# A Hymba layer on one core: the input projection with two products per weight tile in place of three

## The chip, the core and the metric

One core of a Trainium2 chip computes one layer of a hybrid decoder. TensorE (PE in the profile) multiplies; VectorE (DVE), ScalarE (ACT) and GpSimd (POOL) do the elementwise work; SyncE (SP) issues the loads of the weights. The metric is the time of one execution in microseconds (us); less is better.

## The reference

```python
def rms_norm(x, g):
    xf = x.astype(jnp.float32)
    y = xf * lax.rsqrt(jnp.mean(xf * xf, axis=-1, keepdims=True) + EPS)
    return (y * g.astype(jnp.float32)).astype(x.dtype)
...
        xn = rms_norm(h, g_mix[l])
        proj = xn @ w_in[l]
        lru_x, lru_gate, q, kc, vc, ksel, vsel, kw, vw, gate_logits = jnp.split(proj, cuts, axis=-1)
        u = causal_dwconv(lru_x, lru_conv_w[l], lru_conv_b[l])
        y_lru = rg_lru(u, lru_wa[l], lru_ba[l], lru_wx[l], lru_bx[l], lru_lambda[l]) * jax.nn.gelu(lru_gate)
...
        k_cmp = compress_kv(kc, cmp_pe_k[l], cmp_w1_k[l], cmp_b1_k[l], cmp_w2_k[l])
        v_cmp = compress_kv(vc, cmp_pe_v[l], cmp_w1_v[l], cmp_b1_v[l], cmp_w2_v[l])
        y_attn = nsa_attention(q, k_cmp, v_cmp, ksel, vsel, kw, vw, gate_logits)
        mixed = jnp.concatenate([rms_norm(y_lru, g_lru_out[l]), rms_norm(y_attn, g_attn_out[l])], axis=-1)
        h = h + mixed @ w_out[l]
        xn = rms_norm(h, g_ffn[l])
        u_ff, v_ff = jnp.split(xn @ w_up[l], 2, axis=-1)
        u_ff = causal_dwconv(u_ff, ffn_conv_w[l], ffn_conv_b[l])
        h = h + (jax.nn.gelu(u_ff) * v_ff) @ w_down[l]
    return rms_norm(h, g_final)
```

There are 256 tokens, a model width of 2048, eight query heads and two key heads of 128, a recurrent group (RG-LRU) of 1024 channels and a feed-forward width of 6144. All is float32.

## The kernel before

**The weight stream.** The four big matrices (w_in, w_out, w_up, w_down) and the compressor's weights pass once through the chip as a list of *parts*. A part is 1024 weights per partition: in the input projection four tiles of 128 input channels (*contraction tiles*) by 256 output columns. A group of four such parts makes 256 columns of the projection. Loads of one or two parts go through SP into three buffers (`raw`). Each part is split into two float32r halves of 12 bits (`emit_split`): ACT copies the high part (`hi`, L282), DVE subtracts it from the weights (`lo`, L283). There are four buffers of each; splitting runs two parts ahead of the products, loading five. The activations are split in the same way, in tiles `act` with a high and a low part of 256 columns (tokens) side by side.

**The products.** A product of two split numbers leaves out low x low. With the weights standing still and the tokens moving (`mm_weights_still_plain`, L312 to L323, used through `still_x`), a weight tile of 128 x 128 takes three products of 256 columns that add up in the first half of a PSUM bank: high weights x high activations (L320), high x low (L321), low x high (L322). Column tile m has bank m of a pair, and there are two pairs (`ps_mm`). This form serves 16 of the 18 groups of the input projection, 64 parts, 512 weight tiles. The up-projection has another form (`mm_weights_still`): the high weights meet both parts of the activations in one product over a whole bank (512 columns, L336), and the low weights go into its second half (256 columns, L339). Its evictions add the two halves (`halves`, L344 to L348: ACT copies the second half to `ev`, DVE adds the first). The output and down projections move the weights (`moving`, L365 to L367, 512 columns each).

**The order of the groups.** First the compressor's inputs, keys and values by turns (gk, gv); the keys of the selected branch (KS); the keys of the window (KW), by turns with the compressor's weights for keys; the first queries, by turns with the compressor's weights for values; values, the other queries; four groups of recurrent inputs (X) and four of gates (G); then the output projection, its attention rows and its recurrent rows. After a group's last part, `post` evicts its banks: `post_cmp_in` copies them (L418), `post_keys` (L485), `post_q`, `post_lru_x` and `post_lru_g` (L707) multiply them by the tokens' 1/rms, one DVE instruction each.

**Work beside the stream.** Side work (lanes of small tasks) is put between parts. One task sums the squares of x, makes 1/rms per token, and spreads it over the partitions with two products (L200) and a copy to `rsb` (`across`, L202). `blocks` then scales the compressor's inputs and lays out overlapping blocks (POOL, `kvc`, `kb`) and splits them (ACT L432, DVE L433, `kbs`); the compressor's products (L446) read `kbs`. The recurrence (L717 on) starts when the last group of gates has been evicted; its result and the squares of it go into the recurrent rows of the output projection.

**What sets the order.** The program is written in that order, but the Tile scheduler runs with a timeline of its own (`schedule_with_timeline_sim=True`) and orders each engine's instructions by it. So the instructions stand in another order than they are written in, and a change of one kind of work moves others.

Of the kernel before, what the change touches and what calls it, by code (L numbers as in the profile page):

```python
# [15 lines left out]
P = 128  # L16
S = 256            # tokens
NB = S // P        # token blocks
D = 2048
KT = D // P        # contraction tiles of the model width  # L20
# [5 lines left out]
NC = 15            # compressed blocks  # L26
CB = 32            # tokens of a compressed block
CS = 16            # its stride
# [4 lines left out]
LOAD = 2048        # elements per partition of one weight load  # L33
PART = 1024        # elements per partition that are split and multiplied at once
LOOK_LOAD = 5      # parts by which loads run ahead
LOOK_SPLIT = 2     # parts by which the splitting runs ahead
FF_CUT = 3         # the feed-forward width is worked through in so many pieces
PACE = 655         # pace of the side work: units per contraction tile of 256 columns that it is put between
TAIL = 8           # contraction tiles at the end that finish the first token block before the second
# [5 lines left out]
class Part:  # L45
    """A piece of the weight stream: its load, and what is done with it once it is on chip."""

    def __init__(self, load, k0, nk, cols, mm, post):
        self.load, self.k0, self.nk, self.cols = load, k0, nk, cols
        self.mm, self.post, self.pre = mm, post, None  # L50
        self.hi = self.lo = None


class Lane:
    """A queue of side tasks (generators that yield the distance to their next step, in units of PACE)."""
# [22 lines left out]
def hymba_block(ctx, tc, x, g_mix, w_in, lru_conv_w, lru_conv_b, lru_wa, lru_ba, lru_wx, lru_bx, lru_lambda,  # L78
# [23 lines left out]
    # ---------------------------------------------------------------- constants and per-channel vectors  # L102
    ident = cst.tile([P, P], F32, name="ident")
    make_identity(nc, ident)
    xr = resp.tile([P, NB, D], F32, name="xr")           # the residual stream, tokens on partitions
# [8 lines left out]
    # keeps the tensor engine warm until the first operands are there  # L114
# [33 lines left out]
    # a compressed block counts for token t once it has ended: 16 n + 31 <= t  # L148
# [23 lines left out]
    # ---------------------------------------------------------------- helpers  # L172
    def inv_sqrt(v, y):
        """y = 1/sqrt(v) for [P, w]: the reciprocal's root, and a Newton step."""
# [13 lines left out]
    def inv_rms(total, n, name):  # L188
        """1/sqrt(total/n + eps) for [P, w] sums of squares."""
# [753 lines left out]
```

## Time and profile before

| | |
|---|---|
| median of 3 runs | 1186.98 us (1184.58 to 1187.15) |
| span of the profiled execution | 1185.0 us |
| PE busy | 1169.7 us, 99% |
| DVE busy | 766.8 us, 65% |
| ACT busy | 593.1 us, 50% |
| POOL busy | 159.5 us, 13% |
| read from memory | 214.43 MB, 183 GB/s over the span |

A busy share is an average over stages; the chain of work that ended last and the waits of a stretch tell which engine sets the time there. The input projection takes about the first 278 us, the output projection follows to about 350 us, then the feed-forward part runs to the end.

### The profile page before, as it was taken

The page shows a single profiled execution, that of the slowest core. Times are in us where ns is not written, and L with a number is a line of the kernel's source. Part 1 is how long each engine was busy: PE and PEld are TensorE (multiplying, and loading weights), DVE is VectorE, ACT ScalarE, POOL GpSimd, SP SyncE. Part 2 cuts the span into 40 slices and gives each one's busy share as a digit, 9 for nine tenths or more (in the row PEclk, how much of TensorE's full clock was granted, in tenths as well). Part 3 has the DMA queues.
Part 4 walks back from the last instruction along what each step waited for, and adds up shares of the span by engine and source line. Part 5 has one row for each costly group of instructions (what it writes and reads, how often), then busy time and mean ns, then how long its engine had stood idle before and what let it go on. Part 6 is the DMA issues. An engine that isn't in the chain of part 4 may idle for free.

```text
span 1185.0 us, 16730 instructions
## 1 busy us (share of the span) xinstructions
PE 1169.7 (99%) x6727; PEld 1021.5 (86%) x6727; DVE 766.8 (65%) x981; ACT 593.1 (50%) x803; POOL 159.5 (13%) x181
## 2 busy tenths in 40 slices
PE   8999999999999999999999999999999999999997
PEld 8999999898788888888888888888888888888885
DVE  4775778779766766666454766666454666666554
ACT  5554546786446554444333444444333454445444
POOL 3210224113200110110000110110000110110000
PEclk8999999999999999999999999999999999999999
DMA  9676544354655555565556555565555565565562
GB/s 295 178 221 213 160 134 157 121 165 136 217 192 177 176 180 192 176 200 179 204 186 196 179 194 180 178 208 182 187 204 185 176 207 180 178 193 183 194 202 81
DMA packets 182397, 217.60 MB, mean 184 GB/s; under 512 B 4064, under 2 KB 147584, under 8 KB 182192
## 3 DMA queue, kind: packets, MB, share of 16 engines
q1 hardware_dynamic: 180928, 213.07, 55.2%
q0 software_dynamic: 1072, 2.41, 0.6%
q8 instruction: 52, 0.85, 0.3%
q10 hardware_dynamic: 320, 1.06, 0.2%
q14 instruction: 25, 0.20, 0.0%
HBM read 214.43 MB, written 2.10 MB: 183 GB/s over the span
## 4 chain that ended last, share of the span: by engine, by line
PE 91%; DVE 2%; ACT 0%; issue 0%; POOL 0%; DVEq 0%
PE mm L336 30%; PE mm L339 15%; PE mm L366 9%; PE mm L367 9%; PE mm L365 9%; PE mm L322 4%; PE mm L320 4%; PE mm L321 4%; PE s L578 1%; DVE lo L283 1%; PE s L366 1%; PE s L365 1%; PE s L367 1%; PE pt L613 1%; DVE act L223 0%; PE s L604 0%
## 5 line engine op out<-in xcount | busy, mean ns | idle before, releaser
L283 DVE TENSOR_TENSOR lo<-raw,hi 128x1024 fp32r<-128x1024 f32 (+1 forms) x403 | 516.7, 1284 | 294.7 <-ACT hi L282 294.4
L282 ACT ACTIVATE hi<-raw 128x1024 fp32r<-128x1024 f32 (+1 forms) x403 | 424.3, 1055 | 427.7 <-PE mm L367 183.8
L336 PE MATMUL mm<-act,hi 128*128 128x512 f32 x1536 | 539.0, 398 | 0.0
L339 PE MATMUL mm<-act,lo 128*128 128x256 f32 x1536 | 424.2, 281 | 0.0
L336 PEld LDWEIGHTS mm<-act,hi 128*128 128x128 f32 x1536 | 285.7, 188 | 66.6
L339 PEld LDWEIGHTS mm<-act,lo 128*128 128x128 f32 x1536 | 290.6, 189 | 4.5
L366 PE MATMUL mm<-lo,act 128*128 128x512 f32 (+2 forms) x544 | 206.2, 379 | 2.1 <-DVE lo L283 2.1
L367 PE MATMUL mm<-hi,act 128*128 128x512 f32 (+2 forms) x544 | 205.9, 379 | 0.0
L365 PE MATMUL mm<-hi,act 128*128 128x512 f32 (+2 forms) x544 | 205.8, 379 | 0.0
L320 PE MATMUL mm<-act,hi 128*128 128x256 f32 x512 | 147.3, 291 | 1.8 <-ACT act L222 0.9
L322 PE MATMUL mm<-act,lo 128*128 128x256 f32 x512 | 147.9, 290 | 0.6 <-DVE lo L283 0.5
L321 PE MATMUL mm<-act,hi 128*128 128x256 f32 x512 | 147.0, 288 | 0.4 <-DVE act L223 0.4
L366 PEld LDWEIGHTS mm<-lo,act 128*128 128x128 f32 x544 | 102.3, 188 | 22.5 <-DVE lo L283 3.8
L365 PEld LDWEIGHTS mm<-hi,act 128*128 128x128 f32 x544 | 102.3, 188 | 18.9 <-issue 0.4
L367 PEld LDWEIGHTS mm<-hi,act 128*128 128x128 f32 x544 | 102.3, 188 | 18.6
L352 POOL TENSOR_TENSOR up<-up,rsb 128x512 f32<-128x512 f32 x24 | 28.6, 1190 | 593.7 <-DVE up L348 508.4
L320 PEld LDWEIGHTS mm<-act,hi 128*128 128x128 f32 x512 | 98.2, 193 | 4.9 <-issue 2.1
L322 PEld LDWEIGHTS mm<-act,lo 128*128 128x128 f32 x512 | 98.8, 193 | 3.1 <-issue 1.8
L321 PEld LDWEIGHTS mm<-act,hi 128*128 128x128 f32 x512 | 98.9, 194 | 2.2 <-issue 1.2
L347 ACT COPY ev<-mm 128x512 f32<-128x512 f32 x48 | 28.2, 587 | 87.9 <-PE mm L336 87.8
L352 POOL TENSOR_TENSOR cv<-cv,rsb 128x512 f32<-128x512 f32 x24 | 38.7, 1611 | 21.7 <-ACT cv L793 21.7
L348 DVE TENSOR_TENSOR v<-mm,ev 128x512 f32<-128x512 f32 x24 | 16.6, 692 | 29.5 <-ACT ev L347 29.5
(238 smaller groups left out, 740.0 us busy)
## 6 DMA issues: line engine op xcount, KB each, us to landing
raw<-in_w_up_dram SPq DMA_DIRECT2D x96, 1024.0 KB, 5.2
raw<-in_w_down_dram SPq DMA_DIRECT2D x48, 1024.0 KB, 5.1
raw<-in_w_in_dram SPq DMA_DIRECT2D x26, 1024.0 KB, 5.3
raw<-in_w_out_dram SPq DMA_DIRECT2D x16, 1024.0 KB, 5.1
raw<-in_w_in_dram SPq DMA_DIRECT2D x15, 512.0 KB, 5.1
xr<-in_x_dram SPq DMA_DIRECT2D x4, 512.0 KB, 7.5
raw<-in_cmp_w_k_dram SPq DMA_DIRECT2D x4, 512.0 KB, 5.5
raw<-in_cmp_w_v_dram SPq DMA_DIRECT2D x4, 512.0 KB, 5.3
```

The lines of the kernel that those rows point to most:

```text
L282: act(hi[:, :n], src, AF.Copy)
L283: tt(lo[:, :n], src, hi[:, :n].bitcast(F32), op=OP.subtract)
L320: mm(o, lhsT=wh, rhs=a[:, 0], start=k == 0, stop=False)
L321: mm(o, lhsT=wh, rhs=a[:, 1], start=False, stop=False)
L322: mm(o, lhsT=wl, rhs=a[:, 0], start=False, stop=k == kts - 1)
L336: both = lambda: mm(o, lhsT=wh, rhs=a.rearrange("p a s -> p (a s)"), start=k == 0, stop=last)
L339: mm(o[:, S:], lhsT=wl, rhs=a[:, 0], start=False, stop=False)
L347: nc.scalar.copy(t, ps[:, :, S:])
L352: nc.gpsimd.tensor_tensor(a, a, over_pair(shared[rs]), op=OP.mult)
L365: keep(mm(o, lhsT=h, rhs=p.hi[:, j], start=k == 0, stop=False))
L366: mm(o, lhsT=h, rhs=p.lo[:, j], start=False, stop=False)
L367: mm(o, lhsT=l, rhs=p.hi[:, j], start=False, stop=k == kts - 1)
```

## The change

`mm_weights_still_plain` gives way to `mm_weights_still_runs`. It multiplies as the up-projection does: high weights x both parts of the activations over a whole bank, low weights x high activations into the second half. In addition it orders a part's 16 products by kind: eight with high weights, eight with low; a new mark of the part, `lo_first`, lets every other part begin with its low ones, so that runs of neighbouring parts join. Since a bank now has two halves, all evictions of these groups add them: `scaled_halves` (a copy, an add and a multiply by 1/rms), or `halves` alone for the compressor's inputs. Comments have gone from the file too, so line numbers shift by 1 to 14 (L283 is L286 after, L202 is L203, L446 is L460, L717 is L731).

```diff
+        for i, p in enumerate(mine):
+            p.lo_first = i > 0 and (len(mine) - 1 - i) % 2 == 0
...
-    def mm_weights_still_plain(src):
+    def mm_weights_still_runs(src):
         def fn(p, j, k, st, kts):
             if k == 0:
                 st["ps"] = ps_mm.tile([P, 2, 512], F32, name="mm")
-            a = src(k)
-            for m in range(2):
-                o = st["ps"][:, m, :S]
-                wh, wl = p.hi[:, j, m * P:(m + 1) * P], p.lo[:, j, m * P:(m + 1) * P]
-                mm(o, lhsT=wh, rhs=a[:, 0], start=k == 0, stop=False)
-                mm(o, lhsT=wh, rhs=a[:, 1], start=False, stop=False)
-                mm(o, lhsT=wl, rhs=a[:, 0], start=False, stop=k == kts - 1)
+            tiles = [(i, m) for i in range(p.nk) for m in range(2)]
+            order = [(low,) + t for low in ((True, False) if p.lo_first else (False, True)) for t in tiles]
+            n = len(order) // p.nk
+            for low, i, m in order[j * n:(j + 1) * n]:
+                o, kk = st["ps"][:, m], p.k0 + i
+                a = src(kk)
+                w = (p.lo if low else p.hi)[:, i, m * P:(m + 1) * P]
+                if low:
+                    mm(o[:, S:], lhsT=w, rhs=a[:, 0], start=False, stop=False)
+                else:
+                    mm(o, lhsT=w, rhs=a.rearrange("p a s -> p (a s)"), start=kk == 0, stop=kk == kts - 1)
         return fn
...
+    def scaled_halves(dst, ps, rs):
+        halves(dst, ps)
+        tt(dst, dst, over_pair(shared[rs]), op=OP.mult)
...
-            nc.vector.tensor_copy(kvc[:, which], st["ps"][:, :, :S])
+            halves(kvc[:, which], st["ps"])
...
-            tt(kcat[:, :, br], st["ps"][:, :, :S], over_pair(shared["rsb"]), op=OP.mult)
+            scaled_halves(kcat[:, :, br], st["ps"], "rsb")
...
-            tt(qT[:, 2 * i:2 * i + 2], st["ps"][:, :, :S], over_pair(shared["rsbq"]), op=OP.mult)
+            scaled_halves(qT[:, 2 * i:2 * i + 2], st["ps"], "rsbq")
...
-            tt(xp[:, :, 3:], st["ps"][:, :, :S], over_pair(shared["rsb"]), op=OP.mult)
+            scaled_halves(xp[:, :, 3:], st["ps"], "rsb")
...
-            tt(gt, st["ps"][:, :, :S], over_pair(shared["rsb"]), op=OP.mult)
+            scaled_halves(gt, st["ps"], "rsb")
```

The order moves at three places. The first is DVE around the copy of 1/rms, `rsb`, while KS ends and KW begins (`sp` belongs to constants of the recurrence, `kcat` holds the evicted keys, `kbs` the compressor's blocks). Before:

```order
L537 SCALAR_TENSOR_TENSOR sp_1133<-sp_1133,sp_1131 128x8
L539 SCALAR_TENSOR_TENSOR sp<-sp_1133,sp_1130 128x8
L543 TENSOR_SCALAR sp_1152<-sp 128x8
L544 TENSOR_SCALAR sp4n<-sp 128x8
L202 COPY rsb<-pt 128x256
L283 TENSOR_TENSOR lo<-raw,hi 128x1024
L392 TENSOR_SCALAR rsbq<-rsb 128x256
L485 TENSOR_TENSOR kcat<-mm,rsb 128x2x256
L283 TENSOR_TENSOR lo<-raw,hi 128x1024 x2
L433 TENSOR_TENSOR kbs_160<-kb,kbs_160 128x32x30
```

And now:

```order
L187 TENSOR_TENSOR rs<-rms_r,rms_t 128x2
L409 TENSOR_SCALAR rsh<-rs 128x2
L357 TENSOR_TENSOR kcat<-mm,ev 128x2x256
L286 TENSOR_TENSOR lo<-raw,hi 128x1024 x2
L203 COPY rsb<-pt 128x256
L406 TENSOR_SCALAR rsbq<-rsb 128x256
L362 TENSOR_TENSOR kcat<-kcat,rsb 128x2x256
L286 TENSOR_TENSOR lo<-raw,hi 128x1024 x2
L447 TENSOR_TENSOR kbs_160<-kb,kbs_160 128x32x30
```

The copy of `rsb` (L202, now L203) stood ahead of a split and of the keys' eviction; now it stands behind the keys' add (L357) and two splits.

The second is PE at the same place. `mm_691` (now `mm_602`) is the accumulator of KW, `act` its activations, `hi` and `lo` the weights of a part by number; `s` takes the compressor's products. Before, from inside the compressor's first products on:

```order
L446 MATMUL s_722<-hi_762,kbs0_160 120x256
L446 MATMUL s_722<-lo_763,kbs0_160 120x256
L320 MATMUL mm_691<-act_397,hi_775 128x256
L321 MATMUL mm_691<-act_397,hi_775 128x256
L446 MATMUL s_722<-hi_805,kbs0_160 120x256
L322 MATMUL mm_691<-act_397,lo_776 128x256
```

Now, from the first part of KW on:

```order
L331 MATMUL mm_602<-act_179,hi_526 128x512 x8
L329 MATMUL mm_602<-act_179,lo_527 128x256 x8
L329 MATMUL mm_602<-act_231,lo_599 128x256 x3
L201 MATMUL pt_534<-ident_88,rs_503 128x128 x2
L329 MATMUL mm_602<-act_231,lo_599 128x256 x5
L331 MATMUL mm_602<-act_231,hi_598 128x512 x8
L331 MATMUL mm_602<-act_296,hi_635 128x512 x8
L329 MATMUL mm_602<-act_296,lo_636 128x256 x8
L329 MATMUL mm_602<-act_357,lo_671 128x256 x8
L331 MATMUL mm_602<-act_357,hi_670 128x512 x8
L460 MATMUL s_625<-hi_573,kbs0_160 120x256
L460 MATMUL s_625<-lo_574,kbs0_160 120x256
```

The two products that spread 1/rms (L201) stand behind the first part of KW and three products of its second, and all four parts of KW now come before the first compressor product (L460); before, the fourth (`hi_775`) came among the compressor's.

The third is DVE where the last gates are evicted and the recurrence begins (L717 and L731 are its first step, L724 and L738 the second, L727 and L741 the scan; L224 writes attention's result). Before:

```order
L283 TENSOR_TENSOR lo<-raw,hi 128x1024
L186 TENSOR_TENSOR rsA<-rms_r,rms_t 128x2
L717 SCALAR_TENSOR_TENSOR act<-act 128x4x256 x2
L283 TENSOR_TENSOR lo<-raw,hi 128x1024
L724 TENSOR_TENSOR act<-act 128x4x256 x2
L283 TENSOR_TENSOR lo<-raw,hi 128x1024
L727 SCALAR_TENSOR_TENSOR act<-act 128x256 x8
L283 TENSOR_TENSOR lo<-raw,hi 128x1024
L733 TENSOR_TENSOR gt_2933<-gt_2933,act 128x512
L707 TENSOR_TENSOR gt_3306<-mm,rsb 128x512
```

And now:

```order
L286 TENSOR_TENSOR lo<-raw,hi 128x1024
L224 SCALAR_TENSOR_TENSOR act<-s,vec,act 128x128
L731 SCALAR_TENSOR_TENSOR act<-act 128x4x256
L715 SCALAR_TENSOR_TENSOR act<-act,u 128x2x256
L286 TENSOR_TENSOR lo<-raw,hi 128x1024
L224 SCALAR_TENSOR_TENSOR act<-s,vec,act 128x128
L738 TENSOR_TENSOR act<-act 128x4x256
L714 SCALAR_TENSOR_TENSOR act<-gt_2383,act 128x2x256
L741 SCALAR_TENSOR_TENSOR act<-act 128x256 x3
L286 TENSOR_TENSOR lo<-raw,hi 128x1024
L741 SCALAR_TENSOR_TENSOR act<-act 128x256
```

Between two splits there stood two steps or the whole scan; now single steps stand there, with attention's last steps and those of the LRU gates (L714, L715) among them.

The loads on SP keep their order, and from about 300 us on all engines have the order they had.

## Rows read from the trace of the kernel before

**Rows 1.** The page: busy time by engine, and the chain's shares by engine.

```profile
PE 1169.7 (99%) x6727; PEld 1021.5 (86%) x6727; DVE 766.8 (65%) x981; ACT 593.1 (50%) x803; POOL 159.5 (13%) x181
...
PE 91%; DVE 2%; ACT 0%; issue 0%; POOL 0%; DVEq 0%
```

**Rows 2.** Windows: stretch, length, busy us (instructions) by engine, PEclk, DMA share, GB/s.

```profile
6.00:10.50 4.50, 3.22 (x17) 2.45 (x15) 2.76 (x5) 3.67 (x7) 3.09 (x7) 1.00 1.07 371
10.50:17.50 7.00, 6.49 (x31) 6.31 (x31) 1.91 (x4) 1.53 (x4) 2.28 (x7) 0.51 1.09 344
...
86.00:278.00 192.00, 192.00 (x1478) 181.12 (x1477) 138.31 (x232) 119.87 (x225) 42.02 (x53) 1.00 0.49 158
278.00:306.00 28.00, 25.93 (x110) 19.85 (x109) 28.00 (x34) 14.42 (x19) 15.61 (x15) 1.00 0.50 153
```

**Rows 3.** PE's timeline, last G part (48 products): start us, us, instruction.

```profile
272.08 0.28 PE L320 MATMUL mm<-act,hi 128*128 128x256 f32 x1
...
277.84 0.40 PE L365 MATMUL mm<-hi,act 128*128 128x512 f32 x1
```

**Rows 4.** The chain in order of time, up-projection, 32 weight tiles apart.

```profile
417.31 0.24 PE mm L339 x2
...
428.61 0.24 PE mm L339 x2
```

**Rows 5.** PE's timeline in the up-projection: two 512-column products in a row.

```profile
429.04 0.62 PE L336 MATMUL mm<-act,hi 128*128 128x512 f32 x2
429.50 0.28 PE L339 MATMUL mm<-act,lo 128*128 128x256 f32 x1
```

**Rows 6.** PE's timeline in the output projection: twelve 512-column products.

```profile
325.43 0.39 PE L365 MATMUL mm<-hi,act 128*128 128x512 f32 x1
...
328.15 0.39 PE L365 MATMUL mm<-hi,act 128*128 128x512 f32 x1
```

**Rows 7.** Groups by form: out<-in, shape, count, busy us, mean ns, idle before.

```profile
L347 ACT COPY ev<-mm 128x512 f32<-128x512 f32 x48 | 28.2, 587 | 87.9 <-PE mm L336 87.8
L348 DVE TENSOR_TENSOR up<-mm,ev 128x512 f32<-128x512 f32 x24 | 16.6, 692 | 29.0 <-ACT ev L347 29.0
L733 DVE TENSOR_TENSOR gt<-gt,act 128x512 f32<-128x512 f32 x4 | 2.7, 687 | 0.0
L707 DVE TENSOR_TENSOR gt<-mm,rsb 128x512 f32<-128x512 f32 x4 | 2.7, 682 | 0.1
```

**Rows 8.** Timelines of DVE, ACT and PE, 43 to 70 us.

```profile
43.87 1.23 DVE L283 TENSOR_TENSOR lo<-raw,hi 128x1024 fp32r<-128x1024 f32 x1 [0.20 <-ACT hi L282]
49.22 0.42 DVE L202 COPY rsb<-pt 128x256 f32<-128x256 f32 x1 [0.48 <-PE pt L200]
54.73 1.06 ACT L282 ACTIVATE hi<-raw 128x1024 fp32r<-128x1024 f32 x1 [1.77 <-PE mm L321]
59.09 1.16 DVE L433 TENSOR_TENSOR kbs<-kb,kbs 128x960 fp32r<-128x960 f32 x1 [1.67 <-ACT kbs L432]
60.41 0.28 PE L446 MATMUL s<-hi,kbs 128*120 128x256 f32 x1
66.93 0.28 PE L446 MATMUL s<-lo,kbs 128*120 128x256 f32 x1
67.08 1.16 DVE L433 TENSOR_TENSOR kbs<-kb,kbs 128x960 fp32r<-128x960 f32 x1 [2.36 <-ACT kbs L432]
69.65 0.28 PE L320 MATMUL mm<-act,hi 128*128 128x256 f32 x1
```

**Rows 9.** Around the recurrence: PE's waits (total, times, longest); timelines of ACT and DVE.

```profile
PE mm L366 <- DVE lo L283: 2.1, 4, 0.9
...
252.14 1.28 ACT L730 ACT_TABLE_LOAD   x1
259.04 1.07 ACT L282 ACTIVATE hi<-raw 128x1024 fp32r<-128x1024 f32 x1
269.40 2.36 DVE L717 SCALAR_TENSOR_TENSOR act<-act 128x1024 f32<-128x1024 f32 x2 [0.61 <-PE mm L322]
```

More of the change, by code (lines that the diff above doesn't have):

```diff
@@ L51, in __init__ @@
         self.hi = self.lo = None
+        self.lo_first = False
 class Lane:
@@ L401, in hymba_block @@
     tiles_of = lambda src: (lambda k: src[k // 4][:, k % 4])
-    still_x, move_x = mm_weights_still_plain(tiles_of(xT)), mm_weights_move(tiles_of(xT))
+    still_x, move_x = mm_weights_still_runs(tiles_of(xT)), mm_weights_move(tiles_of(xT))
     kcat = mix.tile([P, KVH, 2, S], F32, name="kcat")
```

## The prediction

> **What bounds the kernel now.** I read the page's shares and its chain first: PE is busy for 99% of the span and carries 91% of the chain of work that ended last [rows 1]. Next the busy time by stretch: from 86 us to 278 us, where most of the input projection runs, PE is busy for all of 192.00 us, while DVE has 138.31 and ACT 119.87 [rows 2]. The time of the changed stage is therefore the number of products times their pitch, except in two places where PE waits: around the compressor (66.93 to 69.65 us, below) and after 278 us, where DVE is busy for the whole 28.00 us and PE for 25.93 [rows 2]. The profiled execution's span is 1185.0 us, 2.0 below the median of 1186.98; I make the sum as differences and put them on the median. A change of 0.2% is 2.4 us, about what a measurement of this kernel can tell from none.
>
> **The products.** 512 weight tiles lose three products of 256 columns and get one of 512 and one of 256. The last 48 old products take 277.84 - 272.08 = 5.76 us [rows 3]: 0.120 us each, 0.360 per weight tile, 2.88 per part of eight tiles. What the two new products cost is seen in the up-projection, which has them already, by turns: 32 tiles take 428.61 - 417.31 = 11.30 us [rows 4], 0.353 per tile. The change also puts eight of a kind in a row. Two 512-column products in a row cost 429.50 - 429.04 = 0.46, so 0.230 each [rows 5]; twelve in the output projection take 2.72, 0.227 each [rows 6]. With the 256-column product at its 0.120 a tile costs 0.350 (taken, from the same line of code), at best 0.347, at worst 0.353 (by turns). The gain is 512 x 0.010 = **5.1 us**, bounds 3.6 and 6.8. A part falls to 2.80.
>
> The Trainium skill, page "TensorE: Matmul & The Clock Gate", section "Back-to-back issue gap", gives the spacing of an isolated warm product as its columns over 2.4 plus 2.5 ns. By that, one product fewer saves 2.5 ns a tile, 1.3 us in all instead of 5.1. The trace disagrees in part: every product here costs 13 to 17 ns above its columns (0.120 against 0.107, 0.227 to 0.230 against 0.213), not 2.5.
>
> **The evictions.** Sixteen groups now need an ACT copy (0.587) and a DVE add (0.692); fourteen of them need a multiply as well (0.687), where one instruction of 0.682 did it before [rows 7]. DVE gets 14 x 0.69 = 9.7 us more (the add stands for the old instruction, the multiply is new), ACT 16 x 0.59 = 9.4. Until 278 us that lies beside PE's work: in 192 us DVE idles for 54 and ACT for 72 [rows 2], and PE has two accumulators of two banks, so a group has 11 us until its own is wanted again. I cost it at nothing. Where this cover is gone, after 278 us, one late multiply and one late copy could show, 1.3 us; that goes into the range. Loads don't enter: their order on SP is the same, and the chain has no transfer in it.
>
> **What the order does at the compressor.** This is the expensive side effect. Before, the row of 1/rms (`rsb`) was copied at 49.22, and the first compressor product stood at 60.41, without a wait: 11.19 us for the chain over POOL's products, ACT's and DVE's split of the blocks, and the last step on DVE (59.09 + 1.16) [rows 8]. In the new order PE makes `rsb` behind the first part of the next group and three products of the next (fence on PE); worse, on DVE the copy stands behind the add of the key group and two more weight splits (fence on DVE). The second of those needs a hi/lo buffer: there are four, compressor parts hold theirs until the blocks are ready, and so it takes the one of the first KW part. Call T the end of the KS group on PE. The first KW part ends at T + 2.8; ACT's and DVE's halves of the split take 1.06 + 1.23 [rows 8], so the copy comes at T + 5.2, and the blocks are there at T + 5.2 + 11.2 = T + 16.4. Up to the first compressor product PE has four parts, 4 x 2.80 + 0.2 = 11.4. PE waits for **5.0 us**; about 2.7 of that shows up earlier already, ahead of the fourth KW part, whose split needs the buffer of the third and which now stands in front of the compressor products and not behind them. The second block of tokens is ready 67.08 - 59.09 = 8.0 us after the first [rows 8], at T + 24.4. PE comes to its products after 32 compressor products, one part and two transposes (3.84 + 2.80 + 0.3), at T + 23.4: another 1.0. Together 6.0, against what the same place costs now: 69.65 - 66.93 = 2.72, less five products of 0.12, so 2.1. **Loss 3.9 us.** Bounds: zero or a gain of 2.1 if the copy slips in before the splits, in which case 60.41 - 49.22 fits as it did; 6 if the chain behind the copy is slowed by the splits beside it.
>
> **The end of the group of gates.** From 278 us DVE is the bound, and the four waits of PE there, 2.1 us [rows 9], are for its splits. They go back to the recurrence, whose first step started at 269.40 [rows 9], 8.4 us before the output projection's first product (277.84, [rows 3]). It starts from the last group's accumulators and projections in both orders, so 1.3 us of eviction could be late. In the new order single steps of the recurrence stand between splits, where pairs or eights stood before (third fence): at most 3.3 us of other work between two splits against 4.7. Against that, attention's last steps have moved some 10 us towards this place; there ACT changes function tables, and between two of its splits it now already goes from 252.14 to 259.04 without one, 6.9 us [rows 9]. I take **0**, between a gain of 2.1 (all waits gone) and a loss of 4 (half of 6.9, since the splits run two parts ahead).
>
> **The first 50 us** have waits for x and its transposes; the products there shrink by the same 0.010 and their order barely changes. Counted with the 5.1, give or take 1.5.
>
> **Sum:** -5.1 + 3.9 + 0 = -1.2, so 1186.98 - 1.2 = **1185.8 us** (a profiled span of 1183.8).
>
> **The rivals.**
> *The compressor wait is absent or the recurrence's goes (faster).* The first: -5.1 + 0 = -5.1, 1181.9. The second with the best pitch: -6.8 + 3.9 - 2.1 = -5.0, 1182.0. For it speaks that the old chain had no wait at 60.41; against it the fence, since engines don't overtake in their own order. 0.30.
> *TensorE's clock falls (slower).* Between 6.0 and 10.5 us PE worked for 3.22 of 4.50 us, in small pieces with waits, and in the next 7.0 us its granted clock was 0.51, the lower level of 1.2 GHz [rows 2]; at half speed that is 7.0 x 0.49 = 3.4 us lost. Two waits of 2.7 and 2.3 us with one part between them make a stretch no better filled. Then -1.2 + 3.4 = +2.2: 1189.2. [...] Against it: the wait at 66.93 left the clock at its upper level. 0.13.
> *ACT's tables hold up the second part of the output projection (slower).* Its split has little room, since four waits there are already for splits; if a table load (1.28 us, [rows 9]) and the steps around it land before it, PE waits for 2 to 4 more: 1188 to 1190. 0.10.
> *Columns alone count (slower).* A product of 512 columns costs what two of 256 do, 2 x 0.120 = 0.240, so the merging saves nothing and the compressor's 3.9 is left: 1190.9. The trace speaks against it, with 0.230 in a row [rows 5] and 0.353 for a whole tile by turns [rows 4]. 0.04. (By the page's formula, above, it would be -1.3 + 3.9 = +2.6, so 1189.6.)
> *Forecast* (sum within 2.4 us of none): 0.43.
>
> **How the numbers follow.** Faster by over 0.2% is the first rival, and slower the next three, 0.27 together; the same is 0.43. The range runs from 1180.5 (the best pitch and no loss: 1186.98 - 6.8 = 1180.2) to 1190.0 (clock or tables), and leaves out some 2 in 10: both slow cases at once, or both gains. Within the forecast alone I expect 1184.6 to 1189.
>
> **What would show it.** Right: in the stretch 86 to 270 us parts of 2.80 us, 512-column products 0.230 apart and 256-column products 0.120 apart; the `rsb` copy on DVE about 5 us after the last KS product, and PE waiting there for 5 to 6 us for `kbs` and `lo`; the waits after 278 us near 2.1. Wrong: a part at 2.85 or more (the pitch), a first compressor product without a wait (the loss), a granted clock under 1.00 after it, or a wait for ACT's splits of over 2 us at the start of the output projection.

## The result: 1.2% slower, and the profile after

The changed kernel takes 1200.36 us (1199.53 to 1200.51, four runs) against 1186.38 for the kernel before: ratio 1.0116, interval 1.0103 to 1.0128. The prediction was 1185.8, between 1180.5 and 1190.0; the time lies 10 us above that range. The profiled span is 1198.5 us, 13.5 above the 1185.0 of before.

Busy time and the chain, as [rows 1]:

```profile
PE 1168.7 (98%) x6215; PEld 993.9 (83%) x6215; DVE 774.0 (65%) x995; ACT 601.1 (50%) x819; POOL 164.8 (14%) x181
...
PE 91%; DVE 4%; ACT 2%; issue 1%; POOL 1%; DMA 1%; SPq 0%; ACTq 0%
```

DVE has 7.2 us and ACT 8.0 us more; somewhat less than the 9.7 and 9.4 forecast. PE is busy for only 1.0 us less, though its products need 5.8 us less (below): most of the 13.5 us are waits, and the rest is in the busy time, as products at the lower clock. PE's waits in the first 330 us (total, times, longest):

```profile
PE mm L379 <- DVE xr L775: 5.1, 1, 5.1
PE mm L331 <- DVE act L224: 3.8, 3, 2.3
PE mm L380 <- DVE lo L286: 3.1, 3, 1.9
PE mm L329 <- DVE lo L286: 1.9, 2, 1.7
PE s L460 <- DVE kbs L447: 1.7, 2, 1.1
PE pt L704 <- ACT u L695: 1.6, 1, 1.6
...
PE mm L331 <- DVE xp L357: 1.1, 1, 1.1
PE s L592 <- DVE act L224: 0.9, 1, 0.9
```

Before, the output projection's were 2.1 in all and 0.9 the longest [rows 9].

**Where the time went.** Every kernel's PE timeline has the same marks: the first product of the values (128x280), the first of the other values (256 columns), the first of the output projection (128x512) and its 145th, with which the recurrent rows begin. Three marks of the changed kernel:

```profile
87.42 0.29 PE L379 MATMUL mm<-hi,act 128*128 128x280 f32 x1
...
282.62 0.39 PE L379 MATMUL mm<-hi,act 128*128 128x512 f32 x1
...
328.04 0.40 PE L379 MATMUL mm<-hi,act 128*128 128x512 f32 x1
```

Before, the second stands at 277.84 ([rows 3]), the other two here:

```profile
85.14 0.29 PE L365 MATMUL mm<-hi,act 128*128 128x280 f32 x1
...
314.53 0.40 PE L365 MATMUL mm<-hi,act 128*128 128x512 f32 x1
```

The table gives for each kernel how much later (+) or earlier (-) than before a stretch made it (us, one profiled execution each), and the median of its runs beside that of the kernel before on the same chip.

| kernel | start to values | one group of queries | to the last gate | output projection, attention rows | after that | median, before's median |
|---|---|---|---|---|---|---|
| changed | +2.3 | -0.4 | +2.9 | +8.7 | 0.0 | 1200.36, 1186.38 |
| e1 three products, new evictions | +0.9 | 0.0 | -0.4 | +7.3 | 0.0 | 1196.02, 1186.67 |
| e2 two products, old evictions | -0.1 | -0.4 | -2.4 | +1.2 | 0.0 | 1182.87, 1186.67 |
| e3 by turns | +6.3 | -0.2 | +1.7 | +11.5 | 0.0 | 1205.54, 1186.67 |
| e4 attention's 1/rms on POOL | +2.4 | -0.4 | +2.9 | +0.4 | 0.0 | 1192.03, 1186.67 |
| e5 = e4, input's 1/rms earlier | +4.1 | -0.4 | +2.9 | +0.4 | 0.0 | 1192.62, 1186.67 |
| e6 = e4, multiplies on POOL | +3.7 | -0.4 | -1.1 | +3.7 | 0.0 | 1192.79, 1186.67 |
| e7 three products by kind | -1.5 | 0.0 | 0.0 | 0.0 | 0.0 | 1185.51, 1186.67 |
| e8 = e5 and e6 | +3.4 | -0.4 | -1.1 | +3.7 | +0.3 | 1194.19, 1186.67 |
| e9 changed, PACE 850 | +0.9 | +0.4 | +7.8 | +1.0 | 0.0 | 1196.27, 1186.43 |
| e10 before, PACE 850 | -1.5 | +0.8 | -0.3 | +6.2 | 0.0 | 1191.84, 1186.43 |
| e11 = e9, first groups old | -2.4 | +0.4 | +10.0 | +0.8 | 0.0 | 1193.70, 1186.43 |
| e12 new form in q and X0 | -1.3 | -0.4 | -0.8 | +2.3 | 0.0 | 1186.25, 1185.96 |
| e13 new form in q and X | -1.5 | -0.4 | -1.4 | +1.8 | 0.0 | 1185.28, 1185.96 |
| e14 new form in q and G | -1.2 | -0.4 | -1.7 | +1.7 | 0.0 | 1184.51, 1185.96 |
| e15 = e14, four splits on POOL | -2.0 | -0.4 | -1.7 | +6.7 | 0.0 | 1189.47, 1186.48 |
| e16 before, four splits on POOL | -2.3 | 0.0 | 0.0 | +4.4 | 0.0 | 1190.21, 1186.48 |
| e17 all remedies | -2.2 | -0.4 | +4.0 | +9.9 | 0.0 | 1198.54, 1186.48 |

The stretches are of one execution: those of e1, e2, e8, e11 and e16 lie 1.4 to 2.3 us from the median of their runs, and the start alone differs by up to 2.3 us without a cause in the order (below).

The column of the one group of queries is the products alone: four parts with nothing late. It gives -0.36, 0.09 a part. In those parts PE's timeline shows the joined runs:

```profile
103.06 2.08 PE L329 MATMUL mm<-act,lo 128*128 128x256 f32 x16
104.97 3.82 PE L331 MATMUL mm<-act,hi 128*128 128x512 f32 x16
108.62 2.08 PE L329 MATMUL mm<-act,lo 128*128 128x256 f32 x16
```

From 103.06 to 108.62 two parts' worth of each kind takes 5.56, 2.78 a part, against 2.88 before. Over 64 parts the products gain 64 x 0.09 = 5.8 us. So the other stretches lose 13.5 + 5.8 = 19.3 us. By stretch, with the gain of the parts in it put back: up to the values 2.3 + 20 x 0.09 = 4.1 (two of these 21 parts are halves), to the last gate 2.9 + 40 x 0.09 = 6.5, the output projection 8.7.

### The profile page after: what moved, and what is told of

Read it like the earlier page. It is cut to its first block, busy times and chain, and to the rows that moved or that the text cites. A ratio compares the mean times of both kernels' runs of the same rounds, so it can differ in the third digit from the quotient of the medians.

```text
span 1198.5 us, 15718 instructions
## 1 busy us (share of the span) xinstructions
PE 1168.7 (98%) x6215; PEld 993.9 (83%) x6215; DVE 774.0 (65%) x995; ACT 601.1 (50%) x819; POOL 164.8 (14%) x181
## 3 DMA queue, kind: packets, MB, share of 16 engines
q10 hardware_dynamic: 320, 1.06, 0.2%
## 4 chain that ended last, share of the span: by engine, by line
PE 91%; DVE 4%; ACT 2%; issue 1%; POOL 1%; DMA 1%; SPq 0%; ACTq 0%
PE mm L345 30%; PE mm L348 15%; PE mm L379 9%; PE mm L380 9%; PE mm L381 9%; PE mm L331 8%; PE mm L329 4%; DVE lo L286 1%; PE s L592 1%; ACT hi L285 1%; PE s L381 1%; PE s L379 1%; PE s L380 1%; PE pt L627 1%; DVE act L224 1%
## 5 line engine op out<-in xcount | busy, mean ns | idle before, releaser
L286 DVE TENSOR_TENSOR lo<-raw,hi 128x1024 fp32r<-128x1024 f32 (+1 forms) x403 | 513.2, 1275 | 288.4 <-ACT hi L285 286.5
L345 PE MATMUL mm<-act,hi 128*128 128x512 f32 x1536 | 538.9, 398 | 0.0
L348 PE MATMUL mm<-act,lo 128*128 128x256 f32 x1536 | 423.9, 281 | 0.0
L345 PEld LDWEIGHTS mm<-act,hi 128*128 128x128 f32 x1536 | 285.6, 188 | 66.7
L348 PEld LDWEIGHTS mm<-act,lo 128*128 128x128 f32 x1536 | 290.1, 189 | 4.5
L331 PE MATMUL mm<-act,hi 128*128 128x512 f32 x512 | 134.8, 406 | 5.3 <-DVE act L224 3.8
L331 PEld LDWEIGHTS mm<-act,hi 128*128 128x128 f32 x512 | 94.2, 192 | 27.1 <-DVE act L224 5.2
L356 ACT COPY ev<-mm 128x512 f32<-128x512 f32 x64 | 37.6, 588 | 104.7 <-PE mm L345 87.5
L329 PE MATMUL mm<-act,lo 128*128 128x256 f32 x512 | 73.0, 287 | 1.9 <-DVE lo L286 1.9
L329 PEld LDWEIGHTS mm<-act,lo 128*128 128x128 f32 x512 | 68.3, 191 | 6.7 <-DVE lo L286 2.3
L357 DVE TENSOR_TENSOR v<-mm,ev 128x512 f32<-128x512 f32 x24 | 16.6, 692 | 29.2 <-ACT ev L356 29.2
L357 DVE TENSOR_TENSOR up<-mm,ev 128x512 f32<-128x512 f32 x24 | 16.6, 692 | 29.0 <-ACT ev L356 29.0
L607 POOL TENSOR_SCALAR pr<-pr,cf 128x128 f32<-128x128 f32 (+1 forms) x16 | 18.9, 1193 | 59.9 <-DVE cf L603 59.9
```

Of the source, the lines that this page charges most:

```text
L286: tt(lo[:, :n], src, hi[:, :n].bitcast(F32), op=OP.subtract)
L329: mm(o[:, S:], lhsT=w, rhs=a[:, 0], start=False, stop=False)
L331: mm(o, lhsT=w, rhs=a.rearrange("p a s -> p (a s)"), start=kk == 0, stop=kk == kts - 1)
L345: both = lambda: mm(o, lhsT=wh, rhs=a.rearrange("p a s -> p (a s)"), start=k == 0, stop=last)
L348: mm(o[:, S:], lhsT=wl, rhs=a[:, 0], start=False, stop=False)
L356: nc.scalar.copy(t, ps[:, :, S:])
```

## The experiments

**Theory A:** the order is at fault. The scheduler's new order puts attention's end and the small chain behind it late, and PE waits for what hangs on it. **Theory B:** the new products themselves lose. **Theory C:** the 9.7 us of additional work on DVE are not hidden where DVE is the bound.

**The halves of the change.** In e1 the weight tile's three products return, two of them into the second half:

```diff
+                mm(o[:, :S], lhsT=wh, rhs=a[:, 0], start=k == 0, stop=False)
+                mm(o[:, S:], lhsT=wh, rhs=a[:, 1], start=False, stop=False)
+                mm(o[:, S:], lhsT=wl, rhs=a[:, 0], start=False, stop=k == kts - 1)
```

> The changed kernel with three products of 256 columns per weight tile, in the old order, of which the second and third go into the bank's second half; the new evictions (copy, add, multiply) stay. Theory A (the order: the chain that makes attention's 1/rms stands late on DVE, so the output projection's first eviction and with it a pair of banks comes late; here that chain ends behind split 92 as in the changed kernel, behind 83 before): 1196 to 1202, with one wait of 3 us or more for L775's tile at the output projection. Theory B (the new products themselves lose, the evictions are hidden): 1186 to 1189. Theory C (the 9.7 us of additional DVE work are not hidden where DVE is the bound): 1190 to 1197, with no single long wait.

In e2 the new products stay and the evictions are the old ones; they leave out the bank's second half, so e2's result is not whole:

```diff
-        halves(dst, ps)
-        tt(dst, dst, over_pair(shared[rs]), op=OP.mult)
+        tt(dst, ps[:, :, :S], over_pair(shared[rs]), op=OP.mult)
```

> The changed kernel with the old evictions of one DVE instruction: the bank's second half is left out of the sums, so the output lacks the smaller products. Theory A (order; the chain of attention's 1/rms ends behind split 92 here too): 1190 to 1199 and a long wait for the output projection's banks. Theory B (the products): 1198 to 1202. Theory C (additional DVE work): that work is gone, so 1181 to 1183, the pitch gain of 5.1 us alone.

Measured: e1 1196.02, ratio 1.008 (1.0065 to 1.0095); e2 1182.87, ratio 0.9977 (0.9967 to 0.9986). Theory B is out: the products alone gain 3.8 us by the medians. (It may be less: e2's ten runs lie at 1182.5 to 1182.9 or at 1185.1 to 1185.4, and the profiled one, of the later kind, is 1.6 shorter than the profile of before.) The evictions alone lose 9.4, nearly all of it at the output projection (+7.3). e1's time lies in the ranges of A and of C; that one long wait stands there speaks for A (PE's waits in e1):

```profile
PE mm L372 <- DVE xr L768: 4.8, 1, 4.8
```

But e2 fits neither theory wholly: the chain of attention's 1/rms is as late in its order as in e1, behind the same number of splits, and costs a wait of only 1.9 us. It ends 22 us after the output projection's first product, in e1 25. So a late place in the order need not cost much; how long the work in front of it takes counts too. And the two halves sum to +5.6 where the whole change measures +14.0: 7 to 8 us belong to the two together.

**By turns.** e3 uses `mm_weights_still` for the input projection, as the up-projection does.

> The changed kernel, but each weight tile's two products stand together (512, then 256 columns), as in the up-projection, not eight of a kind in a row. Theory A: the order around attention's 1/rms is the same (behind split 92 to 93), so 1199 to 1203, 1.5 us of it for the pitch of 0.353 in place of 0.350. A rival (parts that begin with their low weights need the later half of their split first, and this costs): 1188 to 1194.

1205.54, ratio 1.016, above the range expected. Ordering by kind is not what loses; without it the changed kernel is 5 us slower still, more than the pitch explains. 4.0 of it lie in the start and at the compressor, where the granted clock was 0.51 from 62.0 to 65.5 us and 0.52 from 72.0 to 79.0.

**The chain of attention's 1/rms.** On DVE, the changed kernel from 285 us on (start, duration, instruction; the rows between are splits, the recurrence and attention's last steps):

```profile
285.31 0.15 DVE L658 COPY tot<-pt 128x2 f32<-128x2 f32 x1
...
288.85 1.03 DVE L193 TENSOR_SCALAR rms_v<-tot 128x2 f32<-128x2 f32 x1
...
293.31 0.15 DVE L179 RECIPROCAL rms_r<-rms_v 128x2 f32<-128x2 f32 x1
...
302.45 0.13 DVE L184 TENSOR_TENSOR rms_t<-rms_r 128x2 f32<-128x2 f32 x1
...
305.98 0.15 DVE L185 TENSOR_TENSOR rms_t<-rms_t,rms_v 128x2 f32<-128x2 f32 x1
...
307.98 0.58 DVE L186 TENSOR_SCALAR rms_t<-rms_t 128x2 f32<-128x2 f32 x1
...
311.22 0.57 DVE L187 TENSOR_TENSOR rsA<-rms_r,rms_t 128x2 f32<-128x2 f32 x1
311.71 1.21 DVE L286 TENSOR_TENSOR lo<-raw,hi 128x1024 fp32r<-128x1024 f32 x1
312.85 2.71 DVE L775 SCALAR_TENSOR_TENSOR xr<-mm,rsA,xr 128x512 f32<-128x512 f32 x4
```

and PE:

```profile
308.90 0.39 PE L381 MATMUL mm<-hi,act 128*128 128x512 f32 x1
314.39 0.76 PE L379 MATMUL mm<-hi,act 128*128 128x512 f32 x1 [5.10 <-DVE xr L775]
...
319.39 0.40 PE L379 MATMUL mm<-hi,act 128*128 128x512 f32 x1
```

Seven steps on two numbers a partition, under 3 us of work, take 26 us, since they stand behind splits, scans and attention steps in DVE's queue. The output projection's first eviction (L775) needs the last of them; PE's third group needs the pair of banks which that eviction frees. Before, the same chain was over long before anyone asked for it (first step, last step, first eviction):

```profile
262.97 0.15 DVE L644 COPY tot<-pt 128x2 f32<-128x2 f32 x1
...
268.64 0.15 DVE L186 TENSOR_TENSOR rsA<-rms_r,rms_t 128x2 f32<-128x2 f32 x1
...
297.85 1.39 DVE L761 SCALAR_TENSOR_TENSOR xr<-mm,rsA,xr 128x512 f32<-128x512 f32 x2
```

The first eviction stood 20.0 us behind the output projection's first product (277.84); now it stands 30.2 behind it. In the changed kernel's wait the clock falls. The changed kernel's windows (as [rows 2]; PEclk is the third number from the right):

```profile
308.00:312.00 4.00, 1.28 (x6) 0.74 (x4) 4.00 (x7) 1.06 (x1) 4.00 (x5) 1.00 0.75 247
312.00:316.00 4.00, 1.61 (x4) 1.35 (x5) 4.00 (x6) 0.00 (x0) 3.49 (x4) 0.53 0.54 209
```

After the wait twelve products take 319.39 - 314.39 = 5.0 us, where [rows 6] has 2.72: 2.3 more at the lower level, 1.2 GHz. e4 moves the last four steps to POOL:

```diff
-            tt(t, r, r, op=OP.mult)
-            tt(t, t, v, op=OP.mult)
-        ts(t, t, -0.5, 1.5, op0=OP.mult, op1=OP.add)
-        tt(y, r, t, op=OP.mult)
+            eng.tensor_tensor(t, r, r, op=OP.mult)
+            eng.tensor_tensor(t, t, v, op=OP.mult)
+        eng.tensor_scalar(t, t, -0.5, 1.5, op0=OP.mult, op1=OP.add)
+        eng.tensor_tensor(y, r, t, op=OP.mult)
```

> The changed kernel, but the last four small steps of attention's 1/rms (128 x 2) run on POOL and not on DVE, so that they stand behind no split and no step of the recurrence; the first eviction of the output projection then stands behind split 90 on DVE, as before the change. Theory A: the wait of 5.1 us for the bank pair goes, and the half clock behind it: 1189 to 1195. Theory C (DVE's work, not the chain): 1199 to 1201, since the same work on DVE ends at the same time.

1192.03 (1191.46 to 1193.42), 8.3 less than the changed kernel, all of it in the one stretch (+8.7 becomes +0.4). In e4 the chain ends 12 us earlier on POOL, the first eviction starts 10 us earlier on DVE (19.9 behind the first product, as before), and no wait for it is left; PE's 145th product comes at 319.84:

```profile
299.25 0.50 POOL L187 TENSOR_TENSOR rsA<-rms_r,rms_t 128x2 f32<-128x2 f32 x1
...
302.71 1.40 DVE L775 SCALAR_TENSOR_TENSOR xr<-mm,rsA,xr 128x512 f32<-128x512 f32 x2
...
319.84 0.40 PE L379 MATMUL mm<-hi,act 128*128 128x512 f32 x1
```

This is shown, then: theory A holds for 8.3 of the 14 us.

**The stretch of X and G.** The next loss lies between 231 and 241 us. The changed kernel's windows there:

```profile
228.00:232.00 4.00, 3.88 (x20) 2.72 (x19) 3.99 (x8) 3.26 (x7) 2.55 (x3) 1.00 0.67 195
232.00:236.00 4.00, 1.51 (x3) 0.48 (x3) 4.00 (x10) 0.94 (x4) 0.10 (x1) 1.00 0.29 78
236.00:240.00 4.00, 3.06 (x7) 2.30 (x8) 3.96 (x8) 3.30 (x10) 0.00 (x0) 0.65 0.79 253
```

DVE is full for 12 us: the convolution of the last X group (L694), attention's masks and maxima (L594, L595), attention's result (L224), two weight splits, and the evictions of two groups. PE waits three times: 0.9 us for attention's result, 1.6 for a copy on ACT that itself waits for the convolution, 1.1 for the eviction (the last three lines of PE's waits, above). Behind each the weight products stand still, and the clock falls once more (0.65). e6 takes the evictions' multiplies off DVE:

```diff
-        tt(dst, dst, over_pair(shared[rs]), op=OP.mult)
+        nc.gpsimd.tensor_tensor(dst, dst, over_pair(shared[rs]), op=OP.mult)
```

> The kernel with attention's 1/rms on POOL, and in addition the evictions' multiply by 1/rms on POOL (14 instructions off DVE, 9.7 us), as the up-projection has it. The waits of 5.9 us between 231 and 241 us stand where DVE is busy all the time. If DVE's additional work makes them: those waits shrink by at least half, 1187 to 1189.5. If it is only the order in which attention's and the gates' steps stand (which stays nearly the same): 1191 to 1193.

1192.79, no faster than e4, and by the total in the range for order alone. But in its place it did what theory C expects: +2.9 becomes -1.1, 4.0 us regained, the waits between 231 and 241 shrink to one of 1.7, and the clock stays up. They are given back at the output projection (+0.4 becomes +3.7) and 1.3 before the values, where the clock fell (0.50 from 63.8 to 67.2 us).

e13 and e14 go to the same stretch from the other side, on the old form by kind and with attention's 1/rms on POOL. Both have the new form in three groups of queries; e13 also in X, e14 in G. e12 has it in the queries and one X group, and the 1/rms on DVE. (The cut is from e13.)

```diff
-    still_x, move_x = mm_weights_still_runs(tiles_of(xT)), mm_weights_move(tiles_of(xT))
+    still_x, still_k, move_x = mm_weights_still_runs(tiles_of(xT)), mm_weights_still_kind(tiles_of(xT)), mm_weights_move(tiles_of(xT))
...
-        group(wi, C_G + i * 256, 256, KT, still_x, post_lru_g(i))
+        group(wi, C_G + i * 256, 256, KT, still_k if i in (0, 1, 2, 3) else still_x, post_lru_g(i))
```

> Two products and the new evictions in four groups only, where nothing waited in the changed kernel: three groups of queries and the first X group (16 parts). The other twelve groups have three products by kind and the old evictions. If the gain of 0.09 us a part is real and the losses belong to the other places: 1185.5 (three products by kind everywhere) less 16 x 0.09 = 1.4, so 1183.5 to 1185. If any four groups of new evictions already push attention's steps together: 1188 or more.

> Two products and the new evictions in the queries (three groups) and all four X groups; the first groups, the keys, the first queries and the four G groups as in the old form (by kind); attention's 1/rms on POOL. If the bunched attention steps between 210 and 250 us come with the evictions of X: they stay, 1187 to 1190. If with those of G: they go, 28 x 0.09 = 2.5 less than three products by kind, 1182.5 to 1184.5.

> The same with X and G exchanged: two products and the new evictions in the queries (three groups) and the four G groups, the old form in X. If the waits between 210 and 250 us come with the evictions of G: 1187 to 1190. If with those of X: 1182.5 to 1184.5. Waits in both this and the run before mean that the amount counts, not the place.

1186.25, 1185.28 and 1184.51, each between the two ranges expected of it (e14's at the edge of the lower one). Neither X nor G alone brings the waits: both stretches end early (-1.4, -1.7). Each expected a culprit and there is none; it takes more of the new form together. Whether that is X with G or also the first groups and the keys, which are old here too, is not shown. In all three the output projection takes 1.7 to 2.3 back. e14 is the fastest complete kernel of the study, ratio 0.9991 (0.9982 to 1.0000): too little to call faster.

**Earlier side work.** e9 sets `PACE = 850` in the changed kernel, e10 in the kernel before.

> The changed kernel with one number altered: PACE 850 in place of 655, so that the side work (attention, gates, the norms) is written further ahead in the stream. On DVE attention's 1/rms then ends behind split 80 and not 93, and all steps of the recurrence stand ahead of split 87; the additional evictions and the products are as in the changed kernel. Theory A (the loss comes from where the side work stands): 1182 to 1188. Theory C (the loss comes from the amount of work on DVE): 1196 to 1201.

> The control for the run with PACE 850: the kernel before with the same number. Its order around the output projection hardly moves (attention's 1/rms behind split 82, before 83). If PACE alone brings nothing: 1185 to 1189. If it is worth as much here as in the changed kernel, what that one regains says nothing of the change: below 1180.

1196.27 and 1191.84. e9 lies in theory C's range, but not for its reason: the wait at the output projection is gone (+8.7 becomes +1.0), as theory A says, and a larger one has come in the stretch before (+2.9 becomes +7.8), where several of attention's score products now wait in a row (217 to 223 us) and the granted clock is 0.50 from 221.8 to 232.0. The loss moved; it was not taken away. The control, slower than expected, shows that the number isn't neutral for the old form either (+6.2 at the output projection).

**The start.** e11 adds to e9 the old form in the first two groups.

> The changed kernel with PACE 850, and with three products of 256 columns (by kind) and the old one-instruction copy for the two first groups alone (the compressor's keys and values), whose first product then doesn't need the low part of x. If the start loses because a 512-column product waits for the low part: the compressor's and the values' stretch ends 1 to 1.5 us earlier than with PACE 850 alone, and the total is lower by that. If the start's loss lies elsewhere: the same time within 0.5.

1193.70 against 1196.27, 2.6 less and more than expected; the stretch up to the values is 3.3 shorter. The changed kernel's PE shows the longest of its three waits there, 3.8 us in all:

```profile
8.84 2.16 PE L331 MATMUL mm<-act,hi 128*128 128x512 f32 x4 [2.28 <-DVE act L224]
```

The 512-column product reads both parts of x and has to wait for DVE's low one; the old form begins with the high one. The direction is shown; of the size a part is chance, since the start differs by itself: e16, whose instructions in the first 85 us stand in the order of the kernel before, reaches the values 2.3 us earlier than that kernel's profile, with the clock up sooner (e16's windows; [rows 2] has 0.51 for both together):

```profile
10.50:14.00 3.50, 3.43 (x22) 3.14 (x22) 1.40 (x3) 0.07 (x1) 2.67 (x8) 0.74 1.08 361
14.00:17.50 3.50, 3.50 (x32) 3.50 (x31) 2.08 (x4) 3.05 (x5) 0.00 (x0) 1.00 1.09 325
```

**The compressor.** e5 moves the input's 1/rms to POOL too and writes it earlier.

```diff
-            yield 2000
+            yield 1000
...
-        shared["rs"] = inv_rms(tot, D, "rs")
-        yield 3000
+        shared["rs"] = inv_rms(tot, D, "rs", nc.gpsimd)
+        yield 500
```

> The kernel with attention's 1/rms on POOL, and in addition the input's 1/rms: its four small steps on POOL too, and the squares and the spreading over the partitions written earlier (the lane yields 1000 and 500 in place of 2000 and 3000), so that the copy of rsb stands behind split 16 on DVE and not 18. If the compressor's wait comes from that copy's place: the stretch up to the values' first product ends 2 us earlier than in the kernel before it, 1189.5 to 1190.5 in all. If it comes from the hi/lo buffers alone (four, three of them held): no change, 1191.5 to 1192.5.

1192.62 and +4.1: a miss. The copy of `rsb` does come 2.6 us earlier (53.82 for 56.46), but the fourth KW part has moved behind the compressor products again, and PE meets them with a wait of 3.2 us in one. Behind it the clock falls (e5's window), which at half speed costs 1.7 us:

```profile
65.40:68.80 3.40, 3.40 (x16) 3.40 (x17) 1.54 (x2) 1.06 (x1) 3.40 (x4) 0.50 0.61 173
```

e8 joins e5 and e6.

> The changed kernel with all three: attention's and the input's 1/rms on POOL, the latter earlier, and the evictions' multiplies on POOL. If the causes add: 1185 to 1188, by the sum of what the two runs before it give against the first. If it stays over 1190, one of the causes is taken wrongly.

1194.19: the causes do not add. The wait is 4.0 us in one here, and the clock falls behind it as in e5.

**By kind alone.** e7 is the kernel before, ordered by kind.

> The kernel before with its three products of 256 columns and its evictions, but a part's products ordered by kind (16 with high weights, 8 with low; every other part begins with low). Neither the products' pitch nor the work on DVE changes, and the order of attention's 1/rms stays (behind split 82, before 83). Expected by the account so far: 1186 to 1188.5. A rival, that beginning with low weights makes waits for DVE's later half of the splits: 1190 or more.

1185.51, ratio 0.9995 (0.9985 to 1.0004), half a us under the range expected: the order by kind costs nothing, and the low-first parts make no wait in the stretches (0.0 in each but the start).

**Work off DVE at the output projection.** e15 adds to e14 four low splits on POOL, e16 does so in the kernel before, e17 puts it together with e4 and the old first groups in the changed kernel.

```diff
-        tt(lo[:, :n], src, hi[:, :n].bitcast(F32), op=OP.subtract)
+        (nc.gpsimd.tensor_tensor if getattr(p, "pool_lo", False) else tt)(lo[:, :n], src, hi[:, :n].bitcast(F32), op=OP.subtract)
```

> The kernel with the new form in the queries and the G groups (and attention's 1/rms on POOL), and in addition four of the first eight weight splits of the output projection (the low halves of its parts 2, 4, 6 and 8) on POOL in place of DVE, 4 x 1.2 us off DVE. If the 1.7 us that the mixed form loses again at the output projection come from DVE being the bound there: 1.5 to 3 us faster than without, 1181.5 to 1183.5, faster than the kernel before. If POOL's slower split is late itself: 1184 to 1188.

> The control: the kernel before with the same four splits on POOL. If DVE's stretch at the output projection bounds this kernel too (2.1 us of waits there): 1184.5 to 1186. If POOL's split is late: 1187 or more.

> The changed kernel with attention's 1/rms on POOL, the old form in the two first groups, and the four splits on POOL; the new form stays in all groups from the keys on. By the sum of the single runs: 1192.0, less 2.6 for the start, less up to 2 for the output projection: 1187.5 to 1189.5; the waits between 210 and 250 us stay. Under 1186 would mean that these came from the start's order as well.

1189.47, 1190.21 and 1198.54: all three slower. e15 and e17 lie above every range expected. e16 lies in its range for a late split on POOL (1187 or more), and there a wait of 2.3 us is for POOL's split; the other long waits are for DVE's. PE's waits in e15, and POOL and DVE there:

```profile
PE mm L400 <- DVE lo L286: 6.4, 2, 3.9
```

```profile
278.41 2.69 POOL L286 TENSOR_TENSOR lo<-raw,hi 128x1024 fp32r<-128x1024 f32 x1 [1.16 <-ACT hi L285]
...
288.97 2.72 POOL L286 TENSOR_TENSOR lo<-raw,hi 128x1024 fp32r<-128x1024 f32 x1
...
278.92 3.27 DVE L286 TENSOR_TENSOR lo<-raw,hi 128x1024 fp32r<-128x1024 f32 x1
...
286.84 5.39 DVE L761 TENSOR_TENSOR_SCAN act<-act 128x256 f32<-128x256 f32 x4
...
292.21 1.20 DVE L286 TENSOR_TENSOR lo<-raw,hi 128x1024 fp32r<-128x1024 f32 x1
```

Beside POOL's splits, DVE's own instructions run long: a split takes 3.27 us, against 1.20 for the one at 292.21, and four steps of the scan take 5.39, where eight took 4.75 in the kernel before:

```profile
277.93 4.75 DVE L727 TENSOR_TENSOR_SCAN act<-act 128x256 f32<-128x256 f32 x8
```

PE's two waits, 2.6 and 3.9 us, end with the splits of 278.92 and 292.21. From these rows I estimate 2.1 us of the first and 3.0 of the second to be this lengthening. So four splits on POOL took no time off DVE. Its busy time (third engine) from 270 to 310 us, e14 and then e15:

```profile
270.00:310.00 40.00, 35.94 (x164) 28.83 (x163) 38.07 (x49) 23.97 (x33) 21.81 (x22) 1.00 0.40 135
270.00:310.00 40.00, 33.57 (x142) 27.07 (x141) 38.85 (x43) 21.03 (x29) 29.71 (x23) 0.91 0.36 128
```

The order has a part as well: no split stands between 282 and 292. In e17 one wait is 8.0 us, and the split that ends it, beside POOL's again, took 3.37. These runs therefore leave theory C open for this stretch: DVE was not lighter loaded in e15, and hardly in e16 (39.06 us busy there, 39.46 before).

## Why the prediction was wrong

- **The bound and the products: right.** The pitch was forecast at 0.350 a tile and 2.80 a part, and is 2.78 to 2.79; the gain is 5.8 us instead of 5.1, inside the bounds. Every product costs more than its columns, as the rows of before said; an estimate by the formula of the Trainium skill for an isolated product, page "TensorE: Matmul & The Clock Gate", section "Back-to-back issue gap", gives a gain of 1.3, and here the trace decides.
- **"I cost it at nothing" (the evictions until 278 us): failed.** The cover was read from a mean: DVE idles 54 of 192 us [rows 2]. The 4 us around 234 have none. The stretch to the last gate loses 6.5 us against its pitch gain, of which multiplies off DVE bring back 4.0 (e6).
- **The compressor: right mechanism, too large.** The forecast was 6.0 of waits. The rows of the changed kernel:

```profile
56.46 0.42 DVE L203 COPY rsb<-pt 128x256 f32<-128x256 f32 x1
...
62.85 1.21 PE L329 MATMUL mm<-act,lo 128*128 128x256 f32 x8 [1.72 <-DVE lo L286]
...
67.04 0.38 PE L460 MATMUL s<-hi,kbs 128*120 128x256 f32 x1 [1.13 <-DVE kbs L447]
```

  KS ends at 52.2, so the copy comes at T + 4.3 (forecast 5.2, though its own terms, 2.8 + 1.06 + 1.23, add up to 5.1) and the first compressor product at T + 14.8 (16.4). The waits are the forecast ones, 1.7 ahead of the fourth part, 1.1 at the first blocks and 0.5 at the second, 3.4 in all, each shorter than forecast by 0.5 to 1.2 us. The stretch from KS to the values loses 1.1 + 12 x 0.09 = 2.2, not 3.9 (at the first KS product the changed kernel is 1.2 behind).
- **"The end of the group of gates ... I take 0": the step that failed most.** The text saw attention's last steps move 10 us towards the output projection, but priced only ACT's tables. It did not ask who waits for attention's end: `rsA`, then the first eviction of the output projection, then a pair of banks, then PE. The bound was 4; the stretch lost 8.7, and e4 shows 8.3 of it to be this chain. The work between two splits was also read too small: "at most 3.3 us" are 4.1 in the trace of the changed kernel (L224 0.34, L738 1.23, L714 0.69, three scan steps 1.85).
- **The first 50 us: taken at 0 give or take 1.5, lost about 2.** The wait for both parts of x was not seen, since the trace of before has no 512-column product there.
- **The clock rival: right mechanism, other places.** At the compressor the changed kernel's clock stayed at 1.00, behind waits of 1.7 and 1.1 us. In e5, e6 and e8 it did fall there, behind waits of 3.2, 1.9 and 4.0. In the changed kernel it fell at 237 and 312 us, after waits during which PE worked for 1.51 and 1.28 of 4 us, and the second fall alone cost 2.3 us.
- **The other rivals.** The merged product is not as dear as two (2.78 a part against 2.88); ACT's tables held nothing up: none of the long waits is for ACT's weight splits.

What stays open: why the scheduler lays attention and the recurrence so much later for evictions of 10 us or products shorter by 3%. The runs show that each of the two does it (e1, e2) and that more of both does it more, not by which rule. The split of the 6.5 us between order and load on DVE isn't settled either: e6 speaks for load, but it changed the order too, and e15 and e16 hardly changed DVE's load. What the start loses by the new form and what by chance isn't separated.

## What to carry to other kernels

When a change makes a scheduler reorder, follow every displaced result to the engine that stands still for it: a chain of tiny steps in the queue of a full engine costs what stands between its links, not what it computes. A mean idle share is no cover; look for the fullest few microseconds in which the new work falls. Work moved to another engine is taken off the first only if that one's busy time says so afterwards (e15). A gain in one stretch can be partly given back in the next (e12 to e14: 1.7 to 2.3 us), so time it to the end of that one.

## What the runs showed of the hardware

The first 85 us of the same instruction order took 2.3 us more or less, by when TensorE's granted clock came up (0.51 from 10.5 to 17.5 us in one execution, 0.74 and then 1.00 in another). In e15 POOL's low split of 128x1024 took 2.69 and 2.72 us where DVE's at 292.21 took 1.20; beside POOL's, DVE's split took 3.27 and four of its scan steps 5.39 (rows above). TensorE's clock fell without a wait longer than 1.6 us: in the changed kernel, after 0.9, 1.6 and 1.1 us of waits between 231 and 237 us, the granted clock was 0.65 from 236 to 240.
